# adaLN sums of layer 0: products with ones and small operations as two entries, placed apart

## The chip, the core and the metric

The kernel runs on one core of one Trainium2 chip. The metric is the device time of one execution in microseconds (us). The engines have their own instruction queues, each worked off in order: TensorE (PE; its weight loads have a row of their own, PEld), VectorE (DVE), ScalarE (ACT), GpSimd (POOL) and SyncE (SP), which here issues nearly all loads.

## What is computed

Two layers are applied to x (256 rows by 2048). Both begin with an RMSNorm and an adaLN modulation whose shift and scale come from the condition c:

```python
cond = jax.nn.silu(c)
mod = cond @ ada_w[i] + ada_b[i]                  # ada_w[i]: 2048 x 6144
shift, scale, gate = jnp.split(mod, 3, axis=-1)
h = rms_norm(x, pre_g[i]) * (1 + scale[:, None, :]) + shift[:, None, :]
y = sgu_mixer(h, ...) if i % 2 == 0 else mla_mixer(h, ...)
x = x + gate[:, None, :] * rms_norm(y, post_g[i])
```

Layer 0 is the gated MLP. Its first step is `h @ w_in` with `w_in` of 2048 x 12288 (`sgu_w_in`), of which the first 8192 columns are u and v. Layer 1 is the latent attention. Everything is float32. The change touches only how shift and scale of layer 0 come into the first 8192 columns of that product.

## The kernel before

**Splitting.** A float32 product is made of three matmuls of a rounded type: each operand is split into a high part and the rest (names ending in h and l, or H and L). For a weight, ACT casts the high part (L113) and DVE subtracts it (L114). One weight, `wi_n_k0_k`, is column block n (512 columns) for the two K blocks k and k+1 (K block: 128 of the 2048 rows), 512 KB in one load. It costs PE 12 matmuls: two K blocks, two halves of the 256 rows, three products.

**Ranges and visits.** `h` is not known at the start, since shift and scale need the whole of `ada_w` first. So K is worked off in ranges, STEPS = ((0, 2, 0), (2, 2, 24), (4, 2, 45), (6, 2, 78), (8, 4, 115), (12, 4, 162)): first K block, number of blocks, and how many cells (column block by K block) PE has before it. This text calls them range 0, 2, 4, 6, 8 and 12. A visit `pi_n_k0` adds to column block n the K blocks that are known by then. It needs two PSUM banks, one for each half of the rows (`pi_n_k0_0`, `pi_n_k0_1`), out of four ("mm" in `acc_bank`). So a visit can start when the banks of the visit but one before it have been read out: by a copy on ACT in a column block's first visit (L708), by an addition into `part_n_b` on DVE in later ones (L715).

**adaLN columns of a range.** `ada_range` (L345) gives a list of small steps. For each of the 16 K blocks one step puts a load into the load queue (two or four K blocks share one) and a multiply-add into the stages: DVE multiplies the 128 rows of `ada_w` by the condition's value of each partition and adds them into `acc_ada` (L294 the first, L296 the others; "row" below). The last step, `fin` of `ada_cols` (L338), sums `acc_ada` over the partitions by matmuls with ones on PE (`ada_sums`, L308, result `pada`), and directly after them, in the same step, `ada_put` makes shift and scale from that with three small DVE operations (L332, L334, L336).

**Transposes.** `hT_steps` (L475) follow: for each two K blocks PE transposes x (`ht`, L458), ACT applies shift and scale (`hf`, L483) and casts the high part (`hH`), and DVE makes the rest (`hL`, L490), one weight step apart from each other.

**What sets the order.** Nothing is scheduled by a compiler: the code emits the instructions in the order in which each engine does them. `Stream` (L60 to L138) holds a list of loads and a list of stages. Loads go out up to six stages of loads ahead (RAW_BUFS); the stage of a weight (cast and subtraction) is emitted 2 weights ahead of PE's use of it, from visit 15 on 4 weights ahead; a hook (rows, sums, transposes, modulation) is emitted when its turn in the list comes. `spread(main, extra)` (L141) deals the entries of `extra` evenly among the weights of `main`. In the loop over the visits the entries are the steps of the next range, with APART = 1 empty entry before and behind `fin`, and then the transposes, 22 entries for a range of two K blocks and 23 for one of four:

```python
            apart = [lambda: None] * APART
            spread(todo, items[:-1] + apart + items[-1:] + apart + hT_steps(STEPS[si][0], STEPS[si][1]))
```

The instruction that adds a bank into `part` is not emitted with its visit but deferred to the next weight, behind that weight's stage and the hooks before it.

Of the kernel before, what the change touches and what calls it, by code (L numbers as in the profile page):

```python
# [30 lines left out]
STEPS = ((0, 2, 0), (2, 2, 24), (4, 2, 45), (6, 2, 78), (8, 4, 115), (12, 4, 162))  # L31
# [109 lines left out]
def spread(main, extra):  # L141

    if not main:
        return
    done = 0
    for i, m in enumerate(main):
        m()
        want = -(-len(extra) * (i + 1) // len(main))
        while done < want:
            extra[done]()  # L150
            done += 1
# [3 lines left out]
def tile_trunk(  # L155
# [20 lines left out]
    ST = Stream(nc, wp)  # L176
# [4 lines left out]
    def small(name, n):  # L181
        return sp.tile([P, n], F32, tag="sm", name=name, bufs=16)
# [4 lines left out]
    def aux_bank(name):  # L187
        return pa.tile([P, 512], F32, tag="ax", name=name)
# [116 lines left out]
    def ada_sums(name, n, state):  # L305
        ps = aux_bank(name)
        for j in range(n):
            nc.tensor.matmul(ps[:, j:j + 1], lhsT=state["acc"][:, j * P:(j + 1) * P], rhs=ones[:, 0:1],  # L308
                             start=True, stop=True)
        return ps  # L310

    def ada_turn(name, n, state):

        state["turned"] = []
        for i in range(0, n, 4):
            ps = aux_bank(f"{name}_{i}")
            for j in range(4):
                nc.tensor.transpose(out=ps[:, j * P:(j + 1) * P], in_=state["acc"][:, (i + j) * P:(i + j + 1) * P],  # L318
                                    identity=ident)
            state["turned"].append((i, ps))  # L320

    def ada_rowsums(name, n, state):
        t = small(name, n)
        for i, ps in state.pop("turned"):
            nc.vector.reduce_sum(out=t[:, i:i + 4], in_=ps.rearrange("p (j q) -> p j q", q=P), axis=AX.X)
        return t
# [9 lines left out]
        nc.vector.scalar_tensor_tensor(amul[:, l, ks], t, 1.0, cols[:, 0, g:g + n], op0=ALU.add, op1=ALU.mult)  # L336

    def ada_cols(l, k0, nk, state):  # L338
        def fin():
            ps = (ada_sums if l == 0 else ada_rowsums)(f"pada_{l}_{k0}", 2 * nk, state)  # L340
            ada_put(l, k0, nk, ps[:, 0:nk], ps[:, nk:2 * nk])

        return fin

    def ada_range(l, k0, nk):  # L345

        st = {}
        n = nk * P
        return ada_items(
            f"ada_{l}_{k0}",  # L350
            lambda k, m: [(t, ada_rows(l, k, m, t * D + k0 * P, n)) for t in range(2)],
            2 * n, st) + ([lambda: ST.hook(lambda: ada_turn(f"tada_{l}_{k0}", 2 * nk, st))] if l else []) + [
                lambda: ST.hook(ada_cols(l, k0, nk, st))]

    def ada_gate(l):

# [118 lines left out]
    def hT_steps(k0, nk):  # L475

        f = {}

        def mod(k):
            ps = turned.pop(k)  # L480
            f[k] = slot(f"hf_{k}", (P, 2, 256))
            for i in range(2):
                nc.scalar.activation(f[k][:, i, :], ps[:, i * 256:(i + 1) * 256], AF.Identity,  # L483
                                     bias=shift[:, 0, k + i:k + i + 1], scale=amul[:, 0, k + i:k + i + 1])
            hH[k // 2] = slot(f"hH_{k}", (P, 2, 256), F32R)
            nc.scalar.copy(out=hH[k // 2], in_=f[k])

        def low(k):
            hL[k // 2] = slot(f"hL_{k}", (P, 2, 256), F32R)
            nc.vector.tensor_tensor(out=hL[k // 2], in0=f.pop(k), in1=hH[k // 2].bitcast(F32), op=ALU.subtract)  # L490

        ks = range(k0, k0 + nk, 2)
        lists = [[lambda k=k: turn_hT(k) for k in ks], [lambda k=k: mod(k) for k in ks], [lambda k=k: low(k) for k in ks]]
        steps = []
        for i in range(len(ks) + 2):
            steps.append([lists[j][i - j] for j in (2, 1, 0) if 0 <= i - j < len(ks)])
        return [lambda fs=fs: ST.hook(lambda: [g() for g in fs]) for fs in steps]
# [20 lines left out]
    while cells < 256:  # L518
        have = sum(nk for k0, nk, at in STEPS if at <= cells)
        n = min(order, key=lambda n: (got[n], n))  # L520
        if have == KD:
            n = [m for m in list(range(8, 16)) + list(range(8)) if got[m] < KD][0]
        if got[n] == have:
            n = max(order, key=lambda n: have - got[n])
# [66 lines left out]
    for k in range(KD):  # L591
# [6 lines left out]
        if k == WAT:  # L598
            n = visits[0][0]
# [24 lines left out]
    todo = []  # L624
    si = 1
    ada1 = [f for k0 in range(0, KD, 4) for f in ada_range(1, k0, 4)]
    for n, k0, nk, at in visits:
        while si < len(STEPS) and at >= STEPS[si][2]:
            items = ada_range(0, STEPS[si][0], STEPS[si][1])
            if si == 1:  # L630
                for i, (b, q) in enumerate([(b, q) for q in range(1, 4) for b in range(NB)]):
                    items[i] = lambda f=items[i], b=b, q=q: (f(), ST.hook(lambda: scale_x(b, q)))
            apart = [lambda: None] * APART
            spread(todo, items[:-1] + apart + items[-1:] + apart + hT_steps(STEPS[si][0], STEPS[si][1]))
            todo = []
            si += 1
        todo += w_chunk(f"wi_{n}_{k0}", sgu_w_in, k0, nk, n) if at else []
# [49 lines left out]
    for p in range(8):  # L687
        todo = []
# [769 lines left out]
```

## Time and profile before

| | before |
|---|---|
| time, median of 3 runs | 1133.02 us (1132.65 to 1133.49) |
| profiled execution | 1135.07 us, of which span 1133.3 us |
| TensorE busy | 1105.4 us, 98% of the span |
| VectorE busy | 909.5 us, 80% |
| ScalarE busy | 577.2 us, 51% |
| mean granted TensorE clock | 0.997 of full speed |

The span is the time between the first and the last instruction of the profiled execution. The projection of layer 0 up to its v blocks takes the first part of it; layer 0's sums for shift and scale stand between about 30 and 260 us. In the rows further down, a timeline row is: start in us, duration in us, engine, line, operation, output <- inputs, partitions x elements, how many such in a row, and in brackets how long the engine stood idle before it and what released it. Buffer numbers of the names are left out there, so `wi_6h` is any weight with k = 6, and `pi` any visit. PEclk is the granted clock as a share of full speed.

### The profile page before, as it was taken

The page shows a single profiled execution, that of the slowest core. Times are in us where ns is not written, and L with a number is a line of the kernel's source. Part 1 is how long each engine was busy: PE and PEld are TensorE (multiplying, and loading weights), DVE is VectorE, ACT ScalarE, POOL GpSimd, SP SyncE. Part 2 cuts the span into 40 slices and gives each one's busy share as a digit, 9 for nine tenths or more (in the row PEclk, how much of TensorE's full clock was granted, in tenths as well). Part 3 has the DMA queues.
Part 4 walks back from the last instruction along what each step waited for, and adds up shares of the span by engine and source line. Part 5 has one row for each costly group of instructions (what it writes and reads, how often), then busy time and mean ns, then how long its engine had stood idle before and what let it go on. Part 6 is the DMA issues. An engine that isn't in the chain of part 4 may idle for free.

```text
span 1133.3 us, 15549 instructions
## 1 busy us (share of the span) xinstructions
PE 1105.4 (98%) x5519; PEld 935.9 (83%) x5519; DVE 909.5 (80%) x1211; ACT 577.2 (51%) x833; POOL 23.5 (2%) x50
## 2 busy tenths in 40 slices
PE   5999999999999999999999999999999999999997
PEld 4778887888887888888888888888888999999885
DVE  3889899978888998798888888857978587778765
ACT  3765335354446555555444344447565366466541
POOL 1000000000000000000001000000000000000000
PEclk9999999999999999999999999999999999999999
DMA  9999898998787998788789999982888754345783
GB/s 324 320 323 320 269 358 287 354 320 265 243 296 240 305 291 276 255 259 287 231 292 340 355 377 354 379 291 75 324 284 306 247 177 134 118 159 169 252 323 111
DMA packets 160509, 308.51 MB, mean 272 GB/s; under 512 B 12313, under 2 KB 29312, under 8 KB 160432
## 3 DMA queue, kind: packets, MB, share of 16 engines
q1 hardware_dynamic: 158432, 302.04, 78.2%
q0 software_dynamic: 1968, 5.49, 1.8%
q8 instruction: 43, 0.70, 0.3%
q14 instruction: 34, 0.28, 0.1%
q10 hardware_dynamic: 32, 0.01, 0.0%
HBM read 303.27 MB, written 4.21 MB: 271 GB/s over the span
## 4 chain that ended last, share of the span: by engine, by line
PE 58%; DVE 3%; ACT 3%; issue 1%; DMA 1%; DVEq 0%; ACTq 0%
PE piz L191 15%; PE po L191 15%; PE pm L191 8%; PE pp L191 7%; PE k L191 2%; PE v L191 2%; PE s L191 1%; PE qn L191 1%; PE mix L191 1%; PE o L191 1%; PE qr L191 1%; PE yt L847 1%; DMA wm<-in_mla_w_in_dram 1%; PE h L191 0%; PE tada L318 0%
## 5 line engine op out<-in xcount | busy, mean ns | idle before, releaser
L296 DVE SCALAR_TENSOR_TENSOR acc_ada<-ada,sc,acc_ada 128x1024 f32<-128x1024 f32 (+1 forms) x135 | 148.9, 1103 | 1.0
L296 DVE SCALAR_TENSOR_TENSOR acc_gate<-gate,sc,acc_gate 128x1024 f32<-128x1024 f32 x60 | 76.7, 1278 | 0.0
L715 DVE TENSOR_TENSOR part<-pi,part 128x512 f32<-128x512 f32 x92 | 59.2, 685 | 1.2 <-PE pi L191 1.2
L113 ACT CAST wi_6h<-wi 128x1024 fp32r<-128x1024 f32 x24 | 25.1, 1051 | 39.0 <-DMA wi<-in_sgu_w_in_dram 36.5
L113 ACT CAST wi_8h<-wi 128x1024 fp32r<-128x1024 f32 x24 | 25.2, 1050 | 37.3 <-DMA wi<-in_sgu_w_in_dram 29.3
L113 ACT CAST wi_4h<-wi 128x1024 fp32r<-128x1024 f32 x24 | 25.2, 1051 | 26.8 <-DMA wi<-in_sgu_w_in_dram 23.5
L114 DVE TENSOR_TENSOR wi_10l<-wi,wi_10h 128x1024 fp32r<-128x1024 f32 x24 | 29.4, 1223 | 11.6 <-ACT wi_10h L113 11.4
L114 DVE TENSOR_TENSOR wi_14l<-wi,wi_14h 128x1024 fp32r<-128x1024 f32 x24 | 29.3, 1221 | 7.0 <-ACT wi_14h L113 7.0
L114 DVE TENSOR_TENSOR wi_8l<-wi,wi_8h 128x1024 fp32r<-128x1024 f32 x24 | 29.3, 1222 | 5.3 <-ACT wi_8h L113 5.3
L114 DVE TENSOR_TENSOR wi_6l<-wi,wi_6h 128x1024 fp32r<-128x1024 f32 x24 | 29.3, 1221 | 4.9 <-ACT wi_6h L113 4.8
L114 DVE TENSOR_TENSOR wi_0l<-wi,wi_0h 128x1024 fp32r<-128x1024 f32 x23 | 28.1, 1222 | 4.7 <-ACT wi_0h L113 4.6
L113 ACT CAST wi_2h<-wi 128x1024 fp32r<-128x1024 f32 x24 | 25.2, 1050 | 13.1 <-DMA wi<-in_sgu_w_in_dram 12.5
L114 DVE TENSOR_TENSOR wi_12l<-wi,wi_12h 128x1024 fp32r<-128x1024 f32 x24 | 29.3, 1221 | 2.7 <-ACT wi_12h L113 2.5
L114 DVE TENSOR_TENSOR wi_4l<-wi,wi_4h 128x1024 fp32r<-128x1024 f32 x24 | 29.3, 1222 | 2.6 <-ACT wi_4h L113 2.5
L114 DVE TENSOR_TENSOR wi_2l<-wi,wi_2h 128x1024 fp32r<-128x1024 f32 x24 | 29.3, 1221 | 1.3 <-ACT wi_2h L113 1.3
L113 ACT CAST wi_10h<-wi 128x1024 fp32r<-128x1024 f32 x24 | 25.1, 1045 | 9.9 <-DMA wi<-in_sgu_w_in_dram 6.7
L113 ACT CAST wi_0h<-wi 128x1024 fp32r<-128x1024 f32 x23 | 24.1, 1049 | 10.3 <-DMA wi<-in_sgu_w_in_dram 9.1
L113 ACT CAST wi_12h<-wi 128x1024 fp32r<-128x1024 f32 x24 | 25.2, 1048 | 5.7 <-DMA wi<-in_sgu_w_in_dram 4.0
L728 ACT ACTIVATE part<-part 128x512 f32<-128x512 f32 x16 | 9.9, 632 | 35.2 <-DVE part L715 35.2
L113 ACT CAST wi_14h<-wi 128x1024 fp32r<-128x1024 f32 x24 | 25.1, 1045 | 5.3 <-DMA wi<-in_sgu_w_in_dram 2.9
L191 PE MATMUL pi<-wi_4h,hH 128*128 128x512 f32 x64 | 25.4, 397 | 2.0 <-DVE part L715 1.9
L1286 ACT ACTIVATE sm<-sm,nm 128x128 f32<-128x128 f32 (+1 forms) x32 | 14.3, 448 | 23.5 <-DVE nm L1284 23.3
(695 smaller groups left out, 3788.4 us busy)
## 6 DMA issues: line engine op xcount, KB each, us to landing
wi<-in_sgu_w_in_dram SPq DMA_DIRECT2D x191, 512.0 KB, 5.4
ada<-in_ada_w_dram SPq DMA_DIRECT2D x240, 256.0 KB, 5.4
gate<-in_ada_w_dram SPq DMA_DIRECT2D x64, 512.0 KB, 5.4
wo<-in_sgu_w_out_dram SPq DMA_DIRECT2D x64, 512.0 KB, 6.2
wm<-in_mla_w_in_dram SPq DMA_DIRECT2D x48, 512.0 KB, 5.5
wp<-in_mla_w_out_dram SPq DMA_DIRECT2D x32, 512.0 KB, 5.8
ukv<-in_mla_w_ukv_dram SPq DMA_DIRECT2D x16, 512.0 KB, 5.0
uq<-in_mla_w_uq_dram SPq DMA_DIRECT2D x12, 384.0 KB, 3.5
```

The lines of the kernel that those rows point to most:

```text
L113: self.nc.scalar.copy(out=h, in_=raw)
L114: self.nc.vector.tensor_tensor(out=l[0:rows], in0=raw[0:rows], in1=h[0:rows].bitcast(F32), op=ALU.subtract)
L191: nc.tensor.matmul(o, lhsT=l, rhs=r, start=start, stop=stop)
L296: nc.vector.scalar_tensor_tensor(acc, raw, w, acc, op0=ALU.mult, op1=ALU.add)
L715: nc.vector.tensor_tensor(out=part[n, b], in0=ps, in1=part[n, b], op=ALU.add)
L728: nc.scalar.activation(part[n, b], part[n, b], AF.Gelu)
L847: nc.tensor.transpose(out=ps[:, i * P:(i + 1) * P], in_=u[:, i * P:(i + 1) * P], identity=ident)
L1286: nc.scalar.activation(sm[:, i, :], sm[:, i, :], AF.Exp, bias=nm[:, i:i + 1], scale=scale, accum_out=su[:, i:i + 1])
```

## The change

`ada_cols` returns two steps in the place of one. For layer 0, `begin` emits the products with ones and `put` the three small operations; for layer 1, whose two steps were separate already, nothing changes. In the loop over the visits the list of a range becomes: the rows, two empty entries, `begin`, three empty entries, `put`, one empty entry, the transposes. That is 27 entries for a range of two K blocks and 28 for one of four, and `spread` deals them over the same weights as before. The number of instructions is the same.

```diff
--- before.py
+++ after.py
@@ -336,11 +336,20 @@
         nc.vector.scalar_tensor_tensor(amul[:, l, ks], t, 1.0, cols[:, 0, g:g + n], op0=ALU.add, op1=ALU.mult)
 
     def ada_cols(l, k0, nk, state):
-        def fin():
-            ps = (ada_sums if l == 0 else ada_rowsums)(f"pada_{l}_{k0}", 2 * nk, state)
+
+        name = f"pada_{l}_{k0}"
+
+        def begin():
+            if l == 0:
+                state["sums"] = ada_sums(name, 2 * nk, state)
+            else:
+                ada_turn(f"tada_{l}_{k0}", 2 * nk, state)
+
+        def put():
+            ps = state["sums"] if l == 0 else ada_rowsums(name, 2 * nk, state)
             ada_put(l, k0, nk, ps[:, 0:nk], ps[:, nk:2 * nk])
 
-        return fin
+        return begin, put
 
     def ada_range(l, k0, nk):
 
@@ -349,8 +358,7 @@
         return ada_items(
             f"ada_{l}_{k0}",
             lambda k, m: [(t, ada_rows(l, k, m, t * D + k0 * P, n)) for t in range(2)],
-            2 * n, st) + ([lambda: ST.hook(lambda: ada_turn(f"tada_{l}_{k0}", 2 * nk, st))] if l else []) + [
-                lambda: ST.hook(ada_cols(l, k0, nk, st))]
+            2 * n, st) + [lambda f=f: ST.hook(f) for f in ada_cols(l, k0, nk, st)]
 
     def ada_gate(l):
 
@@ -631,7 +639,8 @@
                 for i, (b, q) in enumerate([(b, q) for q in range(1, 4) for b in range(NB)]):
                     items[i] = lambda f=items[i], b=b, q=q: (f(), ST.hook(lambda: scale_x(b, q)))
             apart = [lambda: None] * APART
-            spread(todo, items[:-1] + apart + items[-1:] + apart + hT_steps(STEPS[si][0], STEPS[si][1]))
+            spread(todo, items[:-2] + apart * 2 + items[-2:-1] + apart * 3 + items[-1:] + apart
+                   + hT_steps(STEPS[si][0], STEPS[si][1]))
             todo = []
             si += 1
         todo += w_chunk(f"wi_{n}_{k0}", sgu_w_in, k0, nk, n) if at else []
```

The first place is the load queue of SP in range 2, just before the visits pi_5_0 to pi_9_0; `wi_n_0_0` are weights, `ada_0_2_k` the loads of adaLN rows k and k+1 for range 2. Before:

```order
L87 DMA wi_5_0_0_292<-in_sgu_w_in_dram 128x2x512
L87 DMA ada_0_2_8_312<-in_ada_w_dram 128x2x256 x2
L87 DMA wi_6_0_0_319<-in_sgu_w_in_dram 128x2x512
L87 DMA ada_0_2_10_343<-in_ada_w_dram 128x2x256 x2
L87 DMA wi_7_0_0_350<-in_sgu_w_in_dram 128x2x512
L87 DMA ada_0_2_12_374<-in_ada_w_dram 128x2x256 x2
L87 DMA wi_8_0_0_379<-in_sgu_w_in_dram 128x2x512
L87 DMA ada_0_2_14_403<-in_ada_w_dram 128x2x256 x2
L87 DMA wi_9_0_0_408<-in_sgu_w_in_dram 128x2x512
```

After:

```order
L87 DMA wi_5_0_0_297<-in_sgu_w_in_dram 128x2x512
L87 DMA ada_0_2_10_319<-in_ada_w_dram 128x2x256 x2
L87 DMA ada_0_2_12_324<-in_ada_w_dram 128x2x256 x2
L87 DMA wi_6_0_0_351<-in_sgu_w_in_dram 128x2x512
L87 DMA ada_0_2_14_355<-in_ada_w_dram 128x2x256 x2
L87 DMA wi_7_0_0_380<-in_sgu_w_in_dram 128x2x512
L87 DMA wi_8_0_0_384<-in_sgu_w_in_dram 128x2x512
L87 DMA wi_9_0_0_408<-in_sgu_w_in_dram 128x2x512
```

The adaLN loads moved ahead: wi_6_0_0 and wi_7_0_0 have two more such loads ahead of them, wi_8_0_0 one more, wi_9_0_0 none.

The second place is PE at the end of range 6's sums; `pada_0_6` are the products with ones, `ht_6` the transposes. Of each weight's 12 matmuls one is shown here. Before:

```order
L191 MATMUL pi_6_2_0_1108<-wi_6_2_2h_1012,hH_2_584 128x512
...
L191 MATMUL pi_7_2_0_1154<-wi_7_2_2h_1057,hH_2_584 128x512
...
L308 MATMUL pada_0_6_1168<-ones_92,acc_ada_0_6_880 128x1 x4
L191 MATMUL pi_7_2_0_1154<-wi_7_2_4h_1083,hH_4_856 128x512
...
L191 MATMUL pi_7_2_1_1161<-wi_7_2_4l_1084,hH_4_856 128x512
L458 MATMUL ht_6_1195<-ident_78,x_0_1_139 128x128
L458 MATMUL ht_6_1195<-ident_78,x_1_1_147 128x128
...
L191 MATMUL pi_8_2_0_1209<-wi_8_2_2h_1102,hH_2_584 128x512
...
L191 MATMUL pi_8_2_0_1209<-wi_8_2_4h_1129,hH_4_856 128x512
```

After:

```order
L191 MATMUL pi_6_2_0_1112<-wi_6_2_2h_1017,hH_2_584 128x512
...
L308 MATMUL pada_0_6_1126<-ones_92,acc_ada_0_6_881 128x1 x4
L191 MATMUL pi_6_2_0_1112<-wi_6_2_4h_1040,hH_4_856 128x512
...
L191 MATMUL pi_7_2_0_1159<-wi_7_2_2h_1062,hH_2_584 128x512
...
L191 MATMUL pi_8_2_0_1204<-wi_8_2_2h_1106,hH_2_584 128x512
...
L466 MATMUL ht_6_1218<-ident_78,x_0_1_139 128x128
L466 MATMUL ht_6_1218<-ident_78,x_1_1_147 128x128
...
L191 MATMUL pi_8_2_0_1204<-wi_8_2_4h_1134,hH_4_856 128x512
```

The products with ones moved forward, from the middle of the visit pi_7_2 to the middle of pi_6_2, and ht_6 back by one weight, from the start of pi_8_2 to its middle. On ACT the readers of ht_6 (`hf_6`, `hH_6`) stand directly before the cast wi_10_2_4h in both.

The third place is DVE in range 8, before the bank sums of part_0 and part_1, on which the visits pi_2_4 and pi_12_4 wait; `ada_0_8_k` are the rows. Before:

```order
L114 TENSOR_TENSOR wi_2_4_6l_1453<-wi_2_4_6_1379,wi_2_4_6h_1452 128x1024
L296 SCALAR_TENSOR_TENSOR acc_ada_0_8_1273<-ada_0_8_10_1397,sc_104,acc_ada_0_8_1273 128x1024
L114 TENSOR_TENSOR wi_12_4_4l_1475<-wi_12_4_4_1401,wi_12_4_4h_1474 128x1024
L715 TENSOR_TENSOR part_0_0_325<-pi_0_4_0_1432,part_0_0_325 128x512
L715 TENSOR_TENSOR part_0_1_327<-pi_0_4_1_1439,part_0_1_327 128x512
L296 SCALAR_TENSOR_TENSOR acc_ada_0_8_1273<-ada_0_8_11_1419,sc_104,acc_ada_0_8_1273 128x1024
L296 SCALAR_TENSOR_TENSOR acc_ada_0_8_1273<-ada_0_8_12_1423,sc_104,acc_ada_0_8_1273 128x1024
L114 TENSOR_TENSOR wi_12_4_6l_1504<-wi_12_4_6_1446,wi_12_4_6h_1503 128x1024
L296 SCALAR_TENSOR_TENSOR acc_ada_0_8_1273<-ada_0_8_13_1449,sc_104,acc_ada_0_8_1273 128x1024
L114 TENSOR_TENSOR wi_13_4_4l_1525<-wi_13_4_4_1468,wi_13_4_4h_1524 128x1024
L715 TENSOR_TENSOR part_1_0_356<-pi_1_4_0_1480,part_1_0_356 128x512
L715 TENSOR_TENSOR part_1_1_358<-pi_1_4_1_1487,part_1_1_358 128x512
```

After:

```order
L114 TENSOR_TENSOR wi_2_4_6l_1461<-wi_2_4_6_1402,wi_2_4_6h_1460 128x1024
L296 SCALAR_TENSOR_TENSOR acc_ada_0_8_1274<-ada_0_8_12_1405,sc_104,acc_ada_0_8_1274 128x1024
L296 SCALAR_TENSOR_TENSOR acc_ada_0_8_1274<-ada_0_8_13_1424,sc_104,acc_ada_0_8_1274 128x1024
L114 TENSOR_TENSOR wi_12_4_4l_1485<-wi_12_4_4_1428,wi_12_4_4h_1484 128x1024
L724 TENSOR_TENSOR part_0_0_331<-pi_0_4_0_1440,part_0_0_331 128x512
L724 TENSOR_TENSOR part_0_1_333<-pi_0_4_1_1447,part_0_1_333 128x512
L296 SCALAR_TENSOR_TENSOR acc_ada_0_8_1274<-ada_0_8_14_1431,sc_104,acc_ada_0_8_1274 128x1024
L114 TENSOR_TENSOR wi_12_4_6l_1510<-wi_12_4_6_1454,wi_12_4_6h_1509 128x1024
L296 SCALAR_TENSOR_TENSOR acc_ada_0_8_1274<-ada_0_8_15_1457,sc_104,acc_ada_0_8_1274 128x1024
L114 TENSOR_TENSOR wi_13_4_4l_1531<-wi_13_4_4_1476,wi_13_4_4h_1530 128x1024
L724 TENSOR_TENSOR part_1_0_362<-pi_1_4_0_1490,part_1_0_362 128x512
L724 TENSOR_TENSOR part_1_1_364<-pi_1_4_1_1497,part_1_1_364 128x512
```

The rows moved ahead of the bank sums: 14 of the 16 rows stand before part_0 where 11 did, and all 16 before part_1 where 14 did.

Elsewhere: the products with ones move one weight earlier in range 2, two in ranges 8 (from before pi_13_4 to before pi_12_4) and 12, and not in range 4, where the last row moves one weight earlier on DVE; the small operations move one weight later on DVE in ranges 6 and 12 and keep their place in the others; ht_8, ht_12 and ht_14 move one weight later on PE, and of their readers on ACT only those of ht_12 and ht_14 move with them; in range 12 one more row stands before part_15, part_3 and part_4, two or three more before the three after these.

## Rows read from the trace of the kernel before

**Rows 1.** Busy time of engines, page part 1: engine, us (share of span) xinstructions

```profile
PE 1105.4 (98%) x5519; PEld 935.9 (83%) x5519; DVE 909.5 (80%) x1211; ACT 577.2 (51%) x833; POOL 23.5 (2%) x50
```

**Rows 2.** TensorE's waits over the whole span: us in total, times, longest us

```profile
PE pi L191 <- DVE part L715: 2.7, 2, 1.9
...
PE pada L308 <- DVE acc_ada L296: 1.1, 1, 1.1
```

**Rows 3.** Stretches by window; the first line names the columns

```profile
core 0: us, PE busy (x) PEld busy (x) DVE busy (x) ACT busy (x) POOL busy (x), PEclk, DMA share, GB/s
45.00:50.00 5.00, 4.97 (x22) 3.70 (x21) 4.72 (x6) 3.32 (x6) 0.00 (x0) 1.00 1.08 371
85.00:90.00 5.00, 5.00 (x18) 3.95 (x17) 3.38 (x7) 4.64 (x9) 0.00 (x0) 0.66 1.08 365
170.00:175.00 5.00, 3.06 (x14) 2.33 (x13) 4.75 (x7) 1.89 (x3) 0.00 (x0) 1.00 1.03 369
```

**Rows 4.** Timeline near 45 us: start, us, instruction, xcount, [idle before <-releaser]

```profile
43.69 1.05 ACT L113 CAST wi_0h<-wi 128x1024 fp32r<-128x1024 f32 x1 [1.80 <-DMA wi<-in_sgu_w_in_dram]
...
45.28 0.19 PEld L191 LDWEIGHTS pi<-wi_0h,hH 128*128 128x128 f32 x1 [0.45 <-ACT part L708]
...
46.58 1.05 ACT L113 CAST wi_0h<-wi 128x1024 fp32r<-128x1024 f32 x1 [0.86 <-DMA wi<-in_sgu_w_in_dram]
```

**Rows 5.** Timeline, TensorE, range 4's products with ones

```profile
83.75 1.02 PE L308 MATMUL pada<-ones,acc_ada 128*128 128x1 f32 x8 [1.09 <-DVE acc_ada L296]
```

**Rows 6.** Timeline around ht_6: small operations of range 6, transposes, a cast

```profile
125.81 0.16 DVE L332 TENSOR_TENSOR shift<-pada,cols 128x2 f32<-128x2 f32 x1 [1.64 <-PE pada L308]
...
128.50 0.60 PE L458 MATMUL ht<-ident,x 128*128 128x128 f32 x4
...
131.80 1.23 DVE L114 TENSOR_TENSOR wi_4l<-wi,wi_4h 128x1024 fp32r<-128x1024 f32 x1 [2.09 <-ACT wi_4h L113]
```

**Rows 7.** Timeline in range 6: two matmuls 12 apart, the sum part_1

```profile
97.62 0.39 PE L191 MATMUL pi<-wi_2h,hH 128*128 128x512 f32 x1
...
99.02 1.28 DVE L715 TENSOR_TENSOR part<-pi,part 128x512 f32<-128x512 f32 x2
...
100.22 0.75 DVE L296 SCALAR_TENSOR_TENSOR acc_ada<-ada,sc,acc_ada 128x512 f32<-128x512 f32 x1
...
100.34 0.39 PE L191 MATMUL pi<-wi_2h,hH 128*128 128x512 f32 x1
```

**Rows 8.** Timeline in range 8: VectorE before the bank sums, visits behind them

```profile
154.13 1.23 DVE L114 TENSOR_TENSOR wi_6l<-wi,wi_6h 128x1024 fp32r<-128x1024 f32 x1 [0.64 <-ACT wi_6h L113]
...
159.10 1.28 DVE L296 SCALAR_TENSOR_TENSOR acc_ada<-ada,sc,acc_ada 128x1024 f32<-128x1024 f32 x1
...
160.29 1.22 DVE L114 TENSOR_TENSOR wi_6l<-wi,wi_6h 128x1024 fp32r<-128x1024 f32 x1
...
163.76 1.28 DVE L715 TENSOR_TENSOR part<-pi,part 128x512 f32<-128x512 f32 x2
...
164.59 0.47 PE L191 MATMUL pi<-wi_4h,hH 128*128 128x512 f32 x1
...
170.28 1.23 DVE L114 TENSOR_TENSOR wi_4l<-wi,wi_4h 128x1024 fp32r<-128x1024 f32 x1 [0.26 <-ACT wi_4h L113]
...
171.43 1.28 DVE L715 TENSOR_TENSOR part<-pi,part 128x512 f32<-128x512 f32 x2
...
172.25 0.47 PE L191 MATMUL pi<-wi_4h,hH 128*128 128x512 f32 x1 [1.94 <-DVE part L715]
...
177.56 1.98 PEld L308 LDWEIGHTS pada<-ones,acc_ada 128*128 128x128 f32 x16
```

**Rows 9.** Timeline in range 12: VectorE behind ht_8, part_3, the visit pi_5_6

```profile
185.65 1.23 DVE L114 TENSOR_TENSOR wi_6l<-wi,wi_6h 128x1024 fp32r<-128x1024 f32 x1 [2.08 <-ACT wi_6h L113]
...
200.59 1.29 DVE L715 TENSOR_TENSOR part<-pi,part 128x512 f32<-128x512 f32 x2
...
202.36 0.39 PE L191 MATMUL pi<-wi_6h,hH 128*128 128x512 f32 x1
```

## The prediction

> **What bounds the kernel now.** I read the page's busy times first, then TensorE's waits, then a few stretches by window, and last the timelines around the five places where layer 0's sums stand. TensorE (PE) is busy 98% of the span and VectorE (DVE) 80% [rows 1], so only what makes PE stand still, or slows its clock, moves the end. PE's waits in layer 0's projection are few: 1.1 us for one of the products with ones, and "pi <- DVE part", two waits for an evacuated bank, 2.7 us together, the longest 1.9 [rows 2]. That is thin ice: around 45 us the 16 DMA engines are full (share 1.08), and from 85 to 90 us DVE and ScalarE (ACT) work 3.38 and 4.64 of 5 us [rows 3]. PE is the bound, with the loads, ACT and DVE close behind it. The profiled execution took 1135.07 us (span 1133.3); the median of the three runs is 1133.02, which is 2.05 less. I add the sum of the change to each as it is.
>
> **The change part by part.** No instruction is added or removed. The lists of the ranges grow from 22 entries to 27 (ranges of two) or from 23 to 28 (ranges of four), and `spread` deals the longer list out over the same weights. Three things follow in the built orders. The rows of the adaLN weights, loads and multiply-adds alike, come earlier among the weights of `sgu_w_in`. The products with ones (pada) come one or two weights earlier on PE in four of the five ranges. And the transposes ht_6, ht_8, ht_12 and ht_14 come one weight (12 matmuls) later on PE, while the ACT instructions that read ht_6 and ht_8 keep their place in ACT's queue. The small operations hardly move on DVE: one weight later in ranges 6 and 12, not at all in the others. What they can win is seen once: in range 6 DVE waits 1.64 us for pada at 125.81, but 6 us later it waits 2.09 us for a cast anyway [rows 6], so that this win is swallowed. I take the ranges in turn.
>
> *Range 2, loads (about 45 us).* Here ACT's casts wait for the loads of their weights and come every 46.58 - 43.69 = 2.89 us, for one weight load and one adaLN load; the bank copies stand between the casts on ACT, and PE waits for one of them (0.45 us at 45.28) [rows 4]. So a load costs 1.44 us of the queue, and PE has no slack. In the new order of SP's queue the loads of wi_6_0_0 and wi_7_0_0 have two more adaLN loads ahead of them than before, wi_8_0_0 one more, and wi_9_0_0 none. If a load lands by its place in the queue, PE comes 2 x 1.44 = 2.9 us late to pi_6_0, and does not get that back at wi_9_0_0, since it still has the work to do. Term A: +2.9 us; from 0 (the order within the queue does not matter) to 2.9. The Trainium skill says on its page "DMA: Bandwidth & Descriptors", section "Two DMAs through the same engine are not ordered", that nothing orders DMAs across the 16 engines; by it a weight load behind two more loads would land less than two loads late, and with half of A the sum below would be 6.0 instead of 7.4 us. No row here shows which it is.
>
> *Range 4 (82 to 90 us).* The last multiply-add of the range stands one weight earlier on DVE and its load two loads earlier, while pada keeps its place on PE. PE's wait of 1.09 us for it [rows 5] goes. Right behind it the granted clock is 0.66 on average from 85 to 90 us: for part of that time it is at the lower of its two levels, 1.2 GHz, and 5 x (1 - 0.66) = 1.7 us are lost [rows 3]. Ahead of it stand that wait and pada's eight narrow products. I take the wait as the cause and both as gone. Term B: -1.1 - 1.7 = -2.8 us; from -2.8 to 0 (the wait comes back at another operation, and the clock falls all the same).
>
> *Range 6, bank waits (97 to 101 us).* One more multiply-add now stands before the sums part_0 to part_2, up to three more before part_3 and part_4. One of this size takes 0.75 us [rows 7]. PE's visit after next needs the bank of part_1: the sum's first half ends at 99.02 + 0.64 = 99.66, and that visit starts at 100.34; the slack is 0.7 us [rows 7]. A and B cancel for PE but not for DVE, whose chain only begins behind the late loads; I put 0.7 us for that, between 0 and A. Term C: 0.75 + 0.7 - 0.7, about +0.7 us; from 0 to 2.9, since the rows before part_3 and part_4 may count.
>
> *ht_6 (128 us).* PE does ht_6 at 128.50; DVE then waits till 131.80 for a cast that ACT has queued behind the reader of ht_6 [rows 6]. That cast, and all that follows it on DVE, now waits for 12 more matmuls, and 12 take 100.34 - 97.62 = 2.72 us [rows 7].
>
> *Range 8, bank waits (154 to 180 us).* From 131.8 to 180 us DVE works without a gap but for three waits for ACT: 0.64 us the first, 0.26 the last, and a shorter one between [rows 8]: DVE sets the pace here. The visit pi_2_4 starts at 164.59, just behind the bank sum part_0 (163.76 + 0.64 = 164.40), and pi_12_4 starts at 172.25, after 1.94 us of waiting for part_1, so neither has any slack [rows 8]. Three more rows now stand before part_0 and two more before part_1, at 160.29 - 159.10 = 1.19 us each [rows 8]. So part_0 comes 2.72 + 3 x 1.19 = 6.3 us later, less what DVE's gaps give back, from 0 to some 1.1 us (those three); I put 0.4. pi_2_4 starts at 170.5; its 24 matmuls take 2 x 2.72 = 5.4 us, to 175.9. pada_0_8, which now stands before pi_12_4, takes 1.98 us by its row at 177.56, to 177.9; part_1's first half is there by then (171.43 + 0.64 + 2.72 + 2.4 - 0.4 = 176.8), so that the old wait is gone. The visit after it, pi_13_4, starts 5.4 us later, at 183.3; before, it started right behind pada, at 177.56 + 1.98 = 179.5 [rows 8]. Term D: +3.8 us; from 3.1 (all gaps of DVE filled) to 4.2 (none).
>
> *Range 12 (183 to 203 us).* The same again. ht_8 comes one weight later, and DVE already waits 2.08 us, till 185.65, for a cast that ACT has queued behind the reader of ht_8 [rows 9]. So DVE comes 2.72 us later, and one more row (1.2 us) stands before part_3: 3.9 us. The slack is what lies between the end of part_3's first half, 200.59 + 0.64 = 201.23, and the visit that needs its bank, at 202.36: 1.1 us [rows 9]. Term E: 3.9 - 1.1 = +2.8 us; from 0 (DVE, which is then ahead of a PE that D made late, has that much to spare) to 3.0. ht_12 and ht_14 come later too, but their readers on ACT moved back with them behind casts, which hide it; without that cover each would be up to 2.7 us more.
>
> The sum: A 2.9 - B 2.8 + C 0.7 + D 3.8 + E 2.8 = 7.4 us. On the profiled execution 1142.5, on the median 1140.4.
>
> **The rivals.** *The clock falls too.* PE's new waits are longer than any that it has in this stretch now: 5.9 us before pi_2_4, and 2.8 us in range 12. For it: the slow stretch behind the wait of 1.09 us [rows 3, 5]. Against it: the clock is 1.00 around the wait of 1.94 us at 172 us [rows 3, 8]. The first fall would be partly covered by the 1.1 us (177.9 - 176.8) that part_1 has to spare; I price one as in range 4, +1.7 us: 1142.1 on the median. The Trainium skill's page "TensorE: Matmul & The Clock Gate", section "HAM oscillation — how this bites in real kernels", says that pauses between bursts of matmuls let the clock fall back; the trace bears that out at one of these two places. Chance 0.18.
>
> *The lag is absorbed.* While DVE waits for ht_6 the loads run on, so that ACT and DVE find their weights ready and make up the late transposes; D loses most of its size, and E's slack covers the rest. What is left is A + B + C = 0.8 and up to 1 us of D: 1133.8 to 1135.0, no change. For it: three gaps of DVE that end with ACT. Against it: they are some 1.1 us in all, and the multiply-adds cannot shrink. Chance 0.16.
>
> *Faster.* The earlier rows end the wait in range 4 and keep the clock up, the order of the loads costs nothing, and DVE's bank sums have more room than the rows show: A, C, D and E are 0 and B alone counts, 1133.0 - 2.8 = 1130.2. It decides from about 6 us of slack at part_0 of range 8. For it: the waits for banks are only 2.7 us in all [rows 2]; against it: part_0 and part_1 are just those that PE waits for. Chance 0.18.
>
> **How the numbers follow.** Forecast 0.48, rivals 0.18, 0.16 and 0.18. The predicted time is the forecast's, 1140.4 us. Its own range: low, with A and C at 0, D 3.1 and E 0, 3.1 - 2.8 = +0.3, or 1133.3; high, with B at 0 and the others as put, 10.2, or 1143.2, and with the clock's 1.7 some 1145. The faster case must be taken in by part: with 1131 as the low end two thirds of it (0.12) are left out, and some 0.05 above 1145. A measurement of this kernel tells about 0.2% (2.3 us) from no change. Faster by more than that: 0.18; within: 0.16; slower: 0.66 (forecast and clock).
>
> **What would show it.** In the changed kernel's profile: PE's wait for pada of range 4 is gone and the clock from 85 to 90 us is 1.00 (B); PE waits over 2 us for ACT's bank copies near 46 us (A); DVE's waits for the casts behind ht_6 and ht_8 grow from 2.1 to 4.8 us (D, E); PE's waits "pi <- DVE part" grow from 2.7 to about 9 us, with one of 4 to 6 us near 165 us and one of 2 to 3 near 203 us. If the bank sums of range 8 come no later than now, the step on the transposes is wrong and the time is near or below 1133. If they come late and the time is still 1133, the loss was made up behind 260 us, where I put nothing.

## The result, and the profile after

The changed kernel takes 1146.76 us in the median of four runs (1144.26 to 1147.30), the kernel before 1132.84 us. The ratio is 1.0115 (95% interval 1.0104 to 1.0127), some 13 us slower (11.8 to 14.4); the two medians lie 13.9 us apart. Slower was right, 1140.4 us was too little, and 1146.8 lies above the range.

The page's busy times, and TensorE's waits (us in total, times, longest us), of the changed kernel:

```profile
PE 1108.1 (97%) x5519; PEld 936.9 (82%) x5519; DVE 910.4 (79%) x1211; ACT 577.4 (50%) x833; POOL 23.5 (2%) x50
...
PE pi L191 <- DVE part L724: 10.3, 6, 5.2
...
PE pi L191 <- ACT part L717: 3.5, 3, 2.1
```

The work is the same as in [rows 1], the span is 1145.5 us. The wait for the products with ones [rows 2] is gone, as forecast. The waits for bank sums grew from 2.7 to 10.3 us (forecast: about 9), and those for ACT's bank copies are new in this list. The same stretches by window as in [rows 3], and two more:

```profile
core 0: us, PE busy (x) PEld busy (x) DVE busy (x) ACT busy (x) POOL busy (x), PEclk, DMA share, GB/s
45.00:50.00 5.00, 2.87 (x13) 2.01 (x13) 3.22 (x5) 2.02 (x3) 0.00 (x0) 1.00 1.06 378
50.00:55.00 5.00, 5.00 (x16) 3.96 (x15) 4.20 (x5) 4.75 (x7) 0.00 (x0) 0.66 0.98 329
85.00:90.00 5.00, 5.00 (x30) 4.32 (x30) 4.94 (x8) 4.58 (x6) 0.00 (x0) 1.00 1.04 374
165.00:170.00 5.00, 1.59 (x4) 1.33 (x5) 4.81 (x6) 2.09 (x2) 0.00 (x0) 0.63 1.03 390
170.00:175.00 5.00, 5.00 (x17) 3.97 (x16) 4.96 (x6) 1.30 (x2) 0.00 (x0) 0.69 1.03 363
```

From 85 to 90 us the granted clock is now 1.00, but it is below 1 in two other places. And the places of [rows 4 to 9] in the timeline after:

```profile
42.19 1.05 ACT L113 CAST wi_0h<-wi 128x1024 fp32r<-128x1024 f32 x1 [1.44 <-DMA wi<-in_sgu_w_in_dram]
...
47.37 1.04 ACT L113 CAST wi_0h<-wi 128x1024 fp32r<-128x1024 f32 x1 [3.15 <-DMA wi<-in_sgu_w_in_dram]
...
48.95 0.50 PE L191 MATMUL pi<-wi_0h,hH 128*128 128x512 f32 x1 [2.13 <-ACT part L717]
...
87.55 0.95 PE L308 MATMUL pada<-ones,acc_ada 128*128 128x1 f32 x8
...
104.32 0.50 PE L191 MATMUL pi<-wi_2h,hH 128*128 128x512 f32 x1 [0.76 <-DVE part L724]
...
135.34 0.60 PE L466 MATMUL ht<-ident,x 128*128 128x128 f32 x4
...
138.63 1.22 DVE L114 TENSOR_TENSOR wi_4l<-wi,wi_4h 128x1024 fp32r<-128x1024 f32 x1 [5.12 <-ACT wi_4h L113]
...
167.58 1.28 DVE L724 TENSOR_TENSOR part<-pi,part 128x512 f32<-128x512 f32 x2
...
168.41 0.76 PE L191 MATMUL pi<-wi_4h,hH 128*128 128x512 f32 x1 [5.22 <-DVE part L724]
...
173.41 0.39 PE L191 MATMUL pi<-wi_6h,hH 128*128 128x512 f32 x1
...
197.61 1.23 DVE L114 TENSOR_TENSOR wi_6l<-wi,wi_6h 128x1024 fp32r<-128x1024 f32 x1 [6.71 <-ACT wi_6h L113]
...
210.90 0.47 PE L191 MATMUL pi<-wi_6h,hH 128*128 128x512 f32 x1 [1.91 <-DVE part L724]
...
214.93 0.47 PE L191 MATMUL pi<-wi_6h,hH 128*128 128x512 f32 x1 [1.02 <-DVE part L724]
```

To be seen: the cast before pi_5_0 waits 3.15 us for its load, and PE behind it 2.13 us (48.95). The products with ones of range 4 start without a wait. DVE waits 5.12 us behind ht_6 (2.09 before) and 6.71 us behind ht_8 (2.08 before). PE waits longest at 168.41, before pi_1_4, where before it had no wait; the 12 matmuls from there to 173.41 take 5.00 us, where 12 took 2.72 [rows 7].

Where the time went can be read from the start of the same matmuls in both timelines. The third column is the same instructions as before, profiled a second time (the run e10_before_again, below).

| PE starts | before | before, again | after | after less before | in this stretch |
|---|---|---|---|---|---|
| ht_2 (range 2) | 57.55 | 57.52 | 62.60 | +5.05 | +5.05 |
| pi_4_2 (ranges 4 and 6) | 105.79 | 105.16 | 109.90 | +4.11 | -0.94 |
| pi_14_4 (range 8) | 185.92 | 185.79 | 195.11 | +9.19 | +5.08 |
| pi_6_6 (range 12) | 210.52 | 210.38 | 223.20 | +12.68 | +3.49 |
| end of the span | 1133.3 | 1133.0 | 1145.5 | +12.2 | -0.5 |

All of it arises in the first 215 us. A profile shows one execution: the two of the kernel before took 2.05 and 1.24 us more than the medians of their runs, that of the changed kernel 0.54 more. So a lag between two profiles can be off by a microsecond or two, and what a change costs is taken from the medians and ratios.

### The profile page after: what moved, and what is told of

Same layout as the page of the kernel before. It is cut to its first block, busy times and chain, and to the rows that moved or that the text cites. A ratio compares the mean times of both kernels' runs of the same rounds, so it can differ in the third digit from the quotient of the medians.

```text
span 1145.5 us, 15550 instructions
## 1 busy us (share of the span) xinstructions
PE 1108.1 (97%) x5519; PEld 936.9 (82%) x5519; DVE 910.4 (79%) x1211; ACT 577.4 (50%) x833; POOL 23.5 (2%) x50
## 4 chain that ended last, share of the span: by engine, by line
PE 60%; DVE 3%; ACT 1%; issue 1%; DMA 0%; DVEq 0%; ACTq 0%
PE piz L191 15%; PE po L191 15%; PE pm L191 10%; PE pp L191 7%; PE k L191 2%; PE v L191 2%; PE s L191 1%; PE qn L191 1%; PE mix L191 1%; PE o L191 1%; PE qr L191 1%; PE yt L856 1%; PE h L191 0%; PE tada L318 0%; PE zT L1333 0%
## 5 line engine op out<-in xcount | busy, mean ns | idle before, releaser
L113 ACT CAST wi_2h<-wi 128x1024 fp32r<-128x1024 f32 x24 | 25.1, 1050 | 14.1 <-DMA wi<-in_sgu_w_in_dram 12.2
L191 PE MATMUL pi<-wi_0h,hH 128*128 128x512 f32 x60 | 24.9, 414 | 3.5 <-ACT part L717 3.5
L191 PE MATMUL pi<-wi_6h,hH 128*128 128x512 f32 x64 | 25.2, 394 | 2.9 <-DVE part L724 2.9
```

The source lines that it names most:

```text
L113: self.nc.scalar.copy(out=h, in_=raw)
L191: nc.tensor.matmul(o, lhsT=l, rhs=r, start=start, stop=stop)
```

## The experiments

All kernels deal the entries of a range by a table instead of one list, so that each kind of entry can be put where it stands before or where it stands after. Each instruction's place in its engine's order is then exactly that of the one kernel or of the other. In the first four, a range has four letters, for the rows, the products with ones, the small operations and the transposes: "o" is the place of the kernel before, "n" that of the changed one. `due(j, list, weights)` is the weight behind which `spread` would deal entry j of a list of that length.

```diff
-            spread(todo, items[:-2] + apart * 2 + items[-2:-1] + apart * 3 + items[-1:] + apart
-                   + hT_steps(STEPS[si][0], STEPS[si][1]))
+            steps = hT_steps(STEPS[si][0], STEPS[si][1])
+            deal(todo, place(len(todo), CFG[STEPS[si][0]], items, steps))
```

**Range 2 alone.**

```diff
+CFG = {2: 'nnnn', 4: 'oooo', 6: 'oooo', 8: 'oooo', 12: 'oooo'}
```

> Range 2 dealt as in the changed kernel, ranges 4 to 12 as before. Theory (the weight loads come later behind adaLN loads, and the clock falls behind PE's waits): PE is 5.0 us late at ht_2 as in the changed kernel, and nothing behind gives it back, since loads, ACT and DVE are late by as much: 1132.8 + 5.0 = 1137.8 us. Rival (the stretch behind 60 us has enough to spare to make the lag up): 1133 to 1135 us.

Measured: 1136.15 us, ratio 1.0027 (1.0015 to 1.0039), 3.1 us slower. PE starts ht_2 at 60.97, 3.4 us late, and the longest of its waits there is this:

```profile
44.59 0.50 PE L229 MATMUL pi<-wi_0h,hH 128*128 128x512 f32 x1 [1.49 <-ACT part L754]
```

The clock stayed at 1.00 from 45 to 55 us. By the times, the cost of this range is what I had priced (2.9). In the profile part of the lag goes away later: against the second profile of before it shrinks from 3.45 us at ht_2 to 1.5 us at the end of the span (1134.5 against 1133.0), since later waits shrink (1.47 instead of 2.20 us before pi_12_4). What lasts is therefore known only as well as the times tell it, 1.7 to 4.4 us. The 5.05 us in the changed kernel hold the fall of the clock too: there the 12 matmuls of pi_5_0 take 4.23 us (48.95 to 53.18), here 2.88 (48.82 to 51.70).

**Range 4 alone.**

```diff
+CFG = {2: 'oooo', 4: 'nnnn', 6: 'oooo', 8: 'oooo', 12: 'oooo'}
```

> Range 4 dealt as in the changed kernel, all others as before. Theory (PE's wait for the products with ones and the fall of the clock behind it both go): 1.2 + 1.7 us less, 1130.0 us, with no stretch at the lower clock. Rival (the fall of the clock has another cause than this wait): only the wait goes, 1131.6 us, and the clock still falls near 85 us.

Measured: 1132.58 us, ratio 0.9998 (0.9988 to 1.0007): nothing. Neither expectation held. The wait for the products with ones is 0.64 us, the clock stays up, and within 17 us PE waits 1.4 us at two bank sums where the first profile of before shows no wait:

```profile
82.62 1.02 PE L346 MATMUL pada<-ones,acc_ada 128*128 128x1 f32 x8 [0.64 <-DVE acc_ada L334]
...
95.69 0.50 PE L229 MATMUL pi<-wi_2h,hH 128*128 128x512 f32 x1 [0.64 <-DVE part L761]
...
99.47 0.50 PE L229 MATMUL pi<-wi_2h,hH 128*128 128x512 f32 x1 [0.77 <-DVE part L761]
```

That 0.64 is less than the 1.09 of [rows 5] doesn't show that the change shortens this wait. In six profiles whose instructions are the same up to it (the two of before, and the runs below on late transposes, early transposes, later rows of range 8, and rows alone) it is 1.09, 0.92, 0.93, 0, 1.11 and 0.59 us.

**Late transposes alone.**

```diff
+CFG = {2: 'oooo', 4: 'oooo', 6: 'ooon', 8: 'ooon', 12: 'oooo'}
```

> Only the transposes of ranges 6 and 8 are dealt as in the changed kernel (ht_6 and ht_8 one weight later on PE, their readers on ACT in their old place); rows, sums and small operations all as before. Theory (the late transposes hold up ACT's casts and with them DVE): DVE waits some 4.8 us instead of 2.1 behind ht_6 and ht_8, PE then waits some 2.4 us before pi_1_4 and 1.6 us in range 12: 1132.8 + 4.0 = 1136.8 us, and 1.7 more if the clock falls. Rival (only the earlier rows make the bank sums late): within 0.5 us of before, 1133 us.

Measured: 1137.59 us, ratio 1.0041 (1.0026 to 1.0056), 4.6 us slower: the theory (1136.8), not the rival. DVE waits as forecast behind both transposes, and PE behind it, though less than the theory had (2.4 us before pi_1_4, 1.6 in range 12):

```profile
133.66 1.23 DVE L114 TENSOR_TENSOR wi_4l<-wi,wi_4h 128x1024 fp32r<-128x1024 f32 x1 [4.81 <-ACT wi_4h L113]
...
159.75 0.47 PE L229 MATMUL pi<-wi_4h,hH 128*128 128x512 f32 x1 [1.53 <-DVE part L761]
...
189.25 1.22 DVE L114 TENSOR_TENSOR wi_6l<-wi,wi_6h 128x1024 fp32r<-128x1024 f32 x1 [4.80 <-ACT wi_6h L113]
...
201.22 0.47 PE L229 MATMUL pi<-wi_6h,hH 128*128 128x512 f32 x1 [0.58 <-DVE part L761]
...
204.74 0.47 PE L229 MATMUL pi<-wi_6h,hH 128*128 128x512 f32 x1 [0.56 <-DVE part L761]
```

PE's waits for bank sums are 6.1 us in all, against 3.7 in the second profile of before, so that the profile shows 2.4 of the 4.6 us. The transposes of range 12 keep their old place in this run.

**The change with the transposes in their old places.**

```diff
+CFG = {2: 'nnoo', 4: 'nnoo', 6: 'nnoo', 8: 'nnoo', 12: 'nnoo'}
```

> The changed kernel with the transposes of all ranges and the small operations in their old places; rows and products with ones in the new ones. Theory (late transposes cost 2.7 us of DVE in range 8, as much in range 12, and the fall of the clock in range 8): 1146 - 2.7 - 2.7 - 1.2 = about 1139.5 us. Rival (the rows alone make the bank sums late): 1145 us or more.

Measured: 1139.21 us, ratio 1.0057 (1.0041 to 1.0074), as the theory had it. About half of the loss (6.6 us by the ratios, 7.5 by the medians) goes with the transposes and the small operations alone. PE's longest wait for a bank sum in range 8 is 2.50 us instead of 5.22, and the clock does not fall.

The other kernels start from the kernel before. `TURN` moves a range's first transposes by so many weights, `SUMS` its products with ones and small operations; `ROWS[k0] = (a, z)` begins a range's rows a places later (at the last row, none) and deals them over a list that is z entries shorter; a plain number in its place is a, with z at 0.

**Early transposes.**

```diff
+TURN = {6: -1, 8: -1, 12: -1}
```

> The kernel before with one edit: the first transposes of ranges 6, 8 and 12 (ht_6, ht_8, ht_12) come one weight earlier on PE, the opposite of what the change does to them. Theory (where these transposes stand sets how long ACT's casts, and with them DVE, stand still): DVE's waits of 2.1 us behind ht_6 and ht_8 shrink to under 0.5, and PE's wait of 1.9 us before pi_12_4 goes: 1132.9 - 1.9 = 1131.0 us. Rival (ACT would wait for the small operations of the range, or DVE for something else, just as long): 1132.9 us, no change.

Measured: 1132.15 us, ratio 0.9992 (0.9982 to 1.0001): at most 2 us gained, not clear of nothing. The first half of the theory holds behind ht_6: there DVE no longer waits for a cast, only for PE's own matmuls. Behind ht_8 the wait has only moved: DVE now waits 1.81 us, one weight later, for a cast behind the reader of ht_10, which keeps its place. The second half does not hold: PE's wait before pi_12_4 stays, at 1.82 us.

```profile
130.73 0.69 DVE L761 TENSOR_TENSOR part<-pi,part 128x512 f32<-128x512 f32 x1 [0.52 <-PE pi L229]
132.09 0.69 DVE L761 TENSOR_TENSOR part<-pi,part 128x512 f32<-128x512 f32 x1 [0.67 <-PE pi L229]
...
143.25 1.23 DVE L114 TENSOR_TENSOR wi_6l<-wi,wi_6h 128x1024 fp32r<-128x1024 f32 x1 [0.29 <-ACT wi_6h L113]
...
169.27 0.47 PE L229 MATMUL pi<-wi_4h,hH 128*128 128x512 f32 x1 [1.82 <-DVE part L761]
...
185.79 1.23 DVE L114 TENSOR_TENSOR wi_6l<-wi,wi_6h 128x1024 fp32r<-128x1024 f32 x1 [1.81 <-ACT wi_6h L113]
```

A lag of 2.7 us on DVE cost 4.6 us in two ranges, and a lead of 2.1 us was lost before it could be used: DVE came to bank sums that PE had not finished (0.52 and 0.67 us of waiting), then to a cast that was late (0.29). At part_11 DVE is 2.91 us earlier than in the first profile of before, PE behind it 2.53, so that 0.4 us of the lead is left.

**The loads of range 2 alone.** In `ada_items` the load and the multiply-add of a row become two entries. The loads go where the change puts them, the multiply-adds stay.

```diff
+EARLY = (2,)
+        q = due(j, old + 5, weights) if k0 in EARLY else r
+            out.append((min(q, r), items[j].load))
+            out.append((r, items[j].hook))
```

> The kernel before, but in range 2 the adaLN loads stand in SP's queue where the changed kernel has them, while the multiply-adds, the sums and the small operations keep their places of before. Theory (the order of the loads makes the weights late): PE 2.2 to 3.5 us late at ht_2, 1135 to 1136 us as in the run with the whole of range 2. Rival (the earlier multiply-adds on DVE hold the weights' buffers or subtractions up): within 0.5 us of before, 1132.9 us.

Measured: 1136.14 us, ratio 1.0029 (1.0018 to 1.0041), the same as the whole of range 2, and PE is 2.4 us late at ht_2 (59.98), as the theory has it. PE waits for ACT's copies again, 2.6 us in three waits, the longest 1.09 us before pi_5_0. So it is the order of the loads; where the multiply-adds and the sums stand plays no part that can be measured.

**Early transposes, rows of range 8 later.**

```diff
+ROWS = {8: 2}
+TURN = {6: -1, 8: -1, 12: -1}
```

> As the run with the early transposes, and the rows of range 8 begin later (two of 23 places at the first, none at the last row), so that fewer of them stand before the bank sums part_10 to part_1. Theory (rows ahead of a bank sum make it late): what is left of PE's waits before pi_2_4 and pi_12_4 goes, up to 0.7 us: 1130.5 us. Rival (DVE has enough room there once the transposes are early): the same as with the early transposes alone, 1131.0 us.

Measured: 1133.98 us, ratio 1.0011 (1.0002 to 1.0020); neither. It is 1.8 us above the run without the later rows, and I can't say why. Its profile doesn't tell: it is 1.0 us late already at 84 us, where the two programs are still the same, by the wait for range 4's products with ones (1.11 us here, none in the other).

**Rows of range 6 later as well.**

```diff
+ROWS = {8: 2, 6: 2}
```

> As the run before it, and the rows of range 6 begin two of 22 places later too, loads and multiply-adds. Theory (from 30 to 105 us the loads set the pace, and adaLN loads ahead of weights make these late): PE's wait of 1.0 us before pi_3_2 goes, 1129.5 us. Rival (the weights there come no earlier, since the loads are only exchanged with each other): no gain over the run before it, 1130.5 us.

Measured: 1131.96 us, ratio 0.9995 (0.9986 to 1.0005): neither time (1129.5 or 1130.5), 2.0 us below the run before it and level with the early transposes alone. The wait before pi_3_2 is gone, as the theory has it. The wait before pi_12_4 still stands (1.46 us): 14 of the 16 rows are still ahead of part_1.

**The rows of ranges 6, 8 and 12 alone.**

```diff
+ROWS = {6: (0, -5), 8: (0, -5), 12: (0, -5)}
```

> The kernel before, with only the rows (loads and multiply-adds) of ranges 6, 8 and 12 dealt as in the changed kernel; range 2, range 4, all sums, small operations and transposes as before. Theory (a row ahead of a bank sum makes it late by 1.2 us, or by 0.7 in range 6, less the slack there): +0.7 to 1.2 us in range 6, +2.4 us in range 8, 0 to 0.3 us in range 12: 1136.0 to 1136.8 us. Rival (without the late transposes DVE has room for the rows): 1133 to 1134 us.

Measured: 1137.13 us, ratio 1.0035 (1.0023 to 1.0047), 4.0 us slower; the theory, a little above its 1136.8. The wait stands before pi_1_4, and the granted clock is 0.66 on average in the window in which it ends:

```profile
160.68 0.47 PE L230 MATMUL pi<-wi_4h,hH 128*128 128x512 f32 x1 [2.67 <-DVE part L762]
...
160.00:165.00 5.00, 4.32 (x12) 3.44 (x13) 4.96 (x6) 1.81 (x2) 0.00 (x0) 0.66 0.97 322
```

**The kernel before, once more.** All tables as before; the order on every engine is that of the kernel before.

> The instructions of the kernel before in the same order on every engine, run and profiled once more, to see what of the stretch at the lower clock at 85 us belongs to the kernel. Theory (it belongs to that one execution; loads set the pace from 75 to 105 us): 1132.9 us, no stretch at the lower clock, and PE waits about 1.0 us for a bank sum before pi_3_2, where the profile of before shows none. Rival (the wait for the products with ones of range 4 makes the clock fall each time): it falls again near 85 us.

Measured: 1133.58 us, ratio 1.0004 (0.9995 to 1.0013), the theory. The clock is 1.00 from 85 to 90 us although PE has waited 0.92 us for the products with ones, and PE waits before pi_3_2:

```profile
83.53 1.02 PE L347 MATMUL pada<-ones,acc_ada 128*128 128x1 f32 x8 [0.92 <-DVE acc_ada L335]
...
85.00:90.00 5.00, 5.00 (x24) 4.12 (x23) 3.39 (x5) 4.79 (x8) 0.00 (x0) 1.00 1.08 365
...
99.55 0.50 PE L230 MATMUL pi<-wi_2h,hH 128*128 128x512 f32 x1 [0.78 <-DVE part L762]
...
172.12 0.47 PE L230 MATMUL pi<-wi_4h,hH 128*128 128x512 f32 x1 [2.20 <-DVE part L762]
```

With the fall, in the first profile of before, PE started the second weight of pi_15_0 1.8 us later than here (89.44 against 87.64), pi_4_2 0.6 us later, and pi_13_4 0.1 us later (179.49 against 179.35). The fall of the clock had cost that execution nothing that lasted.

**Two combinations.** Early transposes, the rows of range 6 begin later, and the rows of range 8 are dealt over a shorter list, so that 13 and not 14 of them stand before part_1 (12 in the second kernel); its sums and small operations come one weight later, which the early ht_8 allows.

```diff
+ROWS = {6: (2, 0), 8: (0, 2)}
+TURN = {6: -1, 8: -1, 12: -1}
+SUMS = {8: 1}
```

> The kernel before with the early transposes of ranges 6, 8 and 12, the first rows of range 6 two places later, and the rows of range 8 dealt over 21 places in the place of 23, so that 13 and not 14 of them stand before part_1, with range 8's sums and small operations one weight later. Theory (one row less ahead of part_1 takes 1.2 us from PE's wait before pi_12_4, and the early ht_8 hides the later sums): 1132.0 - 1.2 = 1130.8 us. Rival (the loads of the weights take over as the bound): 1132.0 us, as with rows of ranges 6 and 8 beginning later.

The second kernel differs from it in one line:

```diff
+ROWS = {6: (2, 0), 8: (0, 3)}
```

> As the combined run, with the rows of range 8 dealt over 20 places: 12 rows stand before part_1, and two behind part_2, just ahead of the sums. Theory: the whole wait before pi_12_4 goes, 1130.0 us. Rival (the last rows now make the sums late, and PE waits for them at the products with ones): 1131 us or more.

Measured: 1130.34 us, ratio 0.9974 (0.9963 to 0.9985), and 1129.98 us, 0.9973 (0.9961 to 0.9984): 2.9 and 3.1 us faster than the kernel before, and faster than all others, as the two theories had it (1130.8 and 1130.0). PE's waits of the second:

```profile
PE pi L230 <- DVE part L762: 0.7, 1, 0.7
...
PE pada L347 <- DVE acc_ada L335: 0.3, 1, 0.3
```

The wait before pi_12_4 is gone in both. The second row less ahead of part_1 brought nothing more that can be measured.

## Why the prediction fell short

**Range 4 (term B) is the step that failed.** I took 2.8 us off for a wait and a fall of the clock that both go. Both went, as the windows of the changed kernel show. But I did not ask what is late next, though the answer stood in [rows 7]: the bank sum of part_1 had 0.7 us of slack, and PE could come no earlier than that. The run on range 4 alone gains nothing (0.9998) and waits 1.4 us at two bank sums; the second profile of before shows one of these waits, 0.78 us, when the clock doesn't fall. Both parts of the term were also taken from one execution. The wait is anything from 0 to 1.11 us in the six profiles with the same instructions up to it, and the clock falls behind it in one of the six, which had made the loss up by 180 us. In the changed kernel the wait goes where PE comes 5.1 us late; with range 2 alone changed it is down to 0.37 us, too. B was worth 0 and not -2.8. My sentence that A and B cancel for PE fails with it: in range 6 PE waits for bank sums (0.62 and 0.76 us) of a DVE that works without a gap from 93.75 us on, 4.0 us later than in the second profile of before (89.77). So A's lag came through, and ranges 4 and 6 took back only 0.9 us of 5.05.

**The clock was the rival, not the rest.** "The clock falls too" had the chance 0.18 and 1.7 us. It fell twice: behind the waits of range 2, where I had not looked for it, and around the wait before pi_1_4, there over two windows (0.63 and 0.69). In the profile that cost 1.4 us in the 12 matmuls from 48.95 on and 2.3 us in those from 168.41 on; what of it lasts to the end these rows do not tell. The timed runs give an estimate: the one with the mean clock 0.997 took 1144.26 us, those with 0.993 to 0.995 took 1146.65 to 1147.30, 2.4 to 3.0 us more. That is one run against three, and runs of the kernel before with one mean clock, 0.998, lie up to 2 us apart (1132.20 to 1134.25). The Trainium skill's page "TensorE: Matmul & The Clock Gate", section "HAM oscillation — how this bites in real kernels", says that pauses between bursts of matmuls let the clock fall; the longest pause here (5.22 us) agrees, and the shorter ones give no rule (below).

**Range 2 (term A) was right.** 2.9 us forecast, 3.1 measured alone, and 3.3 (2.0 to 4.6) by its loads alone. In the profiles of these two runs part of PE's lag goes back at later waits (at the end 1.5 and 0.3 us are left against the second profile of before), which the times do not bear out. The Trainium skill's page "DMA: Bandwidth & Descriptors", section "Two DMAs through the same engine are not ordered", from which I had worked out half of A, says that nothing orders DMAs across the 16 engines. It gives no times; that a load behind two others would come less than two loads late was my own step, and the run on the loads alone speaks against it.

**Ranges 6, 8 and 12 (C, D, E) had the right mechanism.** The two causes could be measured apart: rows ahead of bank sums cost 4.0 us, late transposes 4.6. Forecast were 0.7 + 3.8 + 2.8 = 7.3 for both together. In the changed kernel range 8 took 5.1 and not 3.8, range 12 took 3.5 and not 2.8. In both the wait came one visit earlier than I had put it. In range 8 it is the one before pi_1_4, which needs the bank of part_11. In the trace of before:

```profile
157.90 1.28 DVE L715 TENSOR_TENSOR part<-pi,part 128x512 f32<-128x512 f32 x2
...
158.90 0.39 PE L191 MATMUL pi<-wi_4h,hH 128*128 128x512 f32 x1
```

The first half of that sum ends at 157.90 + 0.64 = 158.54, so it had 0.4 us of slack and two more rows ahead of it. I had looked only at part_0. And the clock's fall around it, 2.3 us, is in the 5.1. Without it more waits might have come in its place: in the run with the old transposes, where the clock stays up, PE waits 2.50 us before pi_1_4 and 1.48 before pi_2_4.

In range 12 PE waits 1.91 us before pi_4_6 and 1.02 before pi_5_6, 2.9 together, where I had only the second. DVE waits 6.71 us behind ht_8, 4.6 more than before where I had 2.7. The other 1.9 are no lag of their own: DVE comes to that wait 7.3 us later than before (190.90 against 183.57), PE to its transposes 9.2 us later besides the one weight.

With B at 0 and the clock's falls at 2.6, the sum is 7.4 + 2.8 + 2.6 = 12.8 us; measured are 13.0 by the ratio and 12.2 between the profiles. That it comes so close is partly luck: by the table ranges 4 and 6 gave 0.9 us back where C had 0.7 more, and in the rows the clock's falls take 1.4 + 2.3 = 3.7 us and not 2.6. The effects of the parts, each measured alone, add up to the same within their intervals: 3.1 (range 2) - 0.2 (range 4) + 4.0 (rows) + 4.6 (transposes) = 11.5. No run has the products with ones, the small operations or the transposes of range 12 alone, and of the clock's falls this sum holds only what the rows alone bring.

**The other rivals fell.** The lag was absorbed only in small part: in the run with late transposes DVE is 2.72 us later behind ht_6 and still 1.9 at part_11; the 0.8 us between are its own waits of before (0.64 and 0.20 us), and the rest of that stretch it works without a gap but for 0.17 us. The faster case needed B, and B was 0. That the small operations hardly move, so that what the change's words promise is its smaller part, fits: no run shows a gain from it.

Three slips in the working change none of this. The 0.45 us at 45.28 in [rows 4] are a wait of the weight load, PEld; PE's own row shows no wait there. The upper end of the absorbed case is 1133.0 + 1.8 = 1134.8, not 1135.0. And the 3.0 at the upper end of E follows from no row; with no slack it would be 3.9.

## What to carry to other kernels

Before a stall is booked as a gain, look for the next thing that the engine would wait for, and take the smaller of the two; here the slack of 0.7 us stood in the same table as the gain of 2.8. An event that a profile shows once, like a fall of the clock or a single wait of 1 us, needs a second execution before it is put into a sum. And where entries are dealt evenly over a list, every entry put in, an empty one too, moves all that stand before and behind it: what counts is which load then stands ahead of which weight, and which row ahead of which bank sum.

## What was unexpected about the hardware

The clock's falls do not follow from one wait alone. They stand behind waits of 1.09 us (the first profile of before), 2.13 and 5.22 us (the changed kernel) and 2.67 us (the rows alone), but not behind 0.92 us at the same place in the same program, nor behind 1.11 us there (later rows of range 8, the same instructions up to it), 1.49 us (range 2 alone), 1.91 us (the changed kernel, before pi_4_6), 2.20 us (before, again) or 2.50 us (the change with the old transposes). What decides between them stays open.

A lag and a lead of one engine are not worth the same. DVE 2.7 us later behind the two transposes cost 4.6 us; DVE 2.1 us earlier behind ht_6 gained 0.9 us, with an interval that reaches zero. The lead was lost where DVE had to wait for PE's matmuls, and behind ht_8 at the next cast that stands behind a transpose.
